# A ring of seven split half tiles instead of six, with other operands and another order at the norms

## The chip, the cores and the metric

The kernel runs on one core of a Trainium2 chip. The metric is the device time of one execution in microseconds (us). Engines are named as in the profile: PE is TensorE (PEld its weight loads), DVE is VectorE, ACT is ScalarE, POOL is GpSimd, and SP issues most of the transfers.

## The reference

One decoder layer over 256 tokens of width 2048, all in float32. Three sublayers, each followed by a layer norm over `ALPHA * x + sublayer(x)`:

```python
x = layer_norm(ALPHA * x + 0.5 * swiglu_ffn(x, ffn1...), ln1_g, ln1_b)      # 2048 -> 5632 -> 2048
u = x @ w_in + b_in                                                         # 2048 -> 3328
q, k, v, conv_in = split(u)
attn_out = sliding_window_attention_with_sinks(q, k, v, attn_sinks)         # 16 heads, 2 KV heads, window 128
conv_out = conformer_conv_group(conv_in, ...)                               # GLU, causal depthwise conv of 31, norm, swish
x = layer_norm(ALPHA * x + concat(attn_out, conv_out) @ w_out + b_out, ln2_g, ln2_b)
x = layer_norm(ALPHA * x + 0.5 * swiglu_ffn(x, ffn2...), ln3_g, ln3_b)
```

where `layer_norm` takes mean and variance over the 2048 features of a token, and `swiglu_ffn` is `(silu(x @ w_gate) * (x @ w_up)) @ w_down`.

## The kernel before

**Numbers.** Each float32 matrix is split into two parts that the matmul takes: `hi`, a rounded copy (written by ACT), and `lo`, what is left (`raw - hi`, written by DVE, or by POOL for some tiles). A product is then three matmuls (`mm3`, L383): hi with hi, hi with lo, lo with hi.

**Weights.** All weights stream from HBM once, in transfers of 1 MB, each two half tiles of 128 by 1024. `RAW_BUFS = 4` raw buffers hold them. `Steps.split` (L113) makes hi and lo of the next half tile. The results live in a ring of `RING` pairs of buffers; `Steps.ahead` (L138) stops the split of half tile n when `n >= min(used + LEAD, done + RING)`: not more than `LEAD` ahead of the last half tile taken, and not before `RING` older ones were released. `pooled` is the set of half tiles whose lo POOL makes; `POOL_FIRST` lists those at the start of the input projection and of the second FFN.

**Order.** The instructions of every engine run in the order in which the program issues them. `Steps.step` (L166) is called after each half tile's matmuls. It counts a clock `now`, runs the pieces of work that `at(delay, work)` had set for this step (first those without `after`), then splits up to two half tiles, then runs the pieces with `after`. So an engine's queue holds, for one step, first the due work, then the split.

**Tokens.** 256 tokens are two blocks of 128. Output projections (`tokens_by`, L417) go chunk by chunk of 512 features: PSUM sums for both blocks, `evacuate` (L262) adds them to the residual `xt` on DVE and takes `bn_stats`. At the end of a sublayer block 1 lags behind: for the last `SKEW` half tiles only block 0's matmuls are issued at first, `finish(0)` issues block 0's norm, then follow block 1's matmuls of the held half tiles, one step each, block 1's last evacuation, and `finish(1)`.

**Norms.** For the two inner norms `finish` is `norm_to_features` (L292). On DVE: `bn_aggr`, `rsqrt` by Newton rounds (waiting xcat subtractions are put between the rounds), then four chunks `z = (xt - mean) * r` (L325). Then, at the steps listed in `LN_AT` as (delay, chunk, what): what 0 is `turn`, four transposes of a chunk on PE into PSUM (L302); what 1 is `scale`, gain and bias on ACT (L310) and the rounded copy into xcat's hi part, also on ACT (L311); what 2 is `settle`, the subtraction for xcat's lo part on DVE (L312). The last norm is `norm_to_rows` (L364), which stores to the output.

**After the norm.** `token_group` (L396) takes the first half tiles of the next weights, `skew` of them first for block 0 alone, then the same for block 1, then the rest for both. In the mixer its result holds k, v and the first two pairs of q heads (`kvq`, L590). Then come features (`in_c`, `in_q`), attention by pairs of heads, the gated convolution input (`glu`, L658), and the convolution as chains of 31 taps on DVE, which are issued so long as a modelled backlog of DVE is below `CAP`. While the mixer and the second FFN start, `residuals` (L333) rebuilds the scaled residual from `xt`; it loads rows of gain, bias and output bias, broadcast over the partitions, into `BC` buffers (`row_chunk`, L257) through SP's queue.

Of the kernel before, what the change touches and what calls it, by code (L numbers as in the profile page):

```python
# [9 lines left out]
F32 = mybir.dt.float32  # L10
# [3 lines left out]
AF = mybir.ActivationFunctionType  # L14
ALU = mybir.AluOpType
# [3 lines left out]
P = 128  # L19
D = 2048  # L20
S = 256
# [8 lines left out]
CK = 31  # L30
# [5 lines left out]

RAW_BUFS = 4
EARLY = 4
RING = 6
LEAD = 5  # L40
SKEW = 6
BC = 6
ORDER = "ccqqccqqccqqcc"
CAP = 4.0
CONV_AT = (1, 3, 1)
HB = 5
POOL_FIRST = (0, 1, 2, 4)
POOL_SPAN = (20, 84)
POOL_SHARE = (4, 7)
ZB = 5  # L50

LN_AT = ((5, 0, 0), (5, 0, 1), (6, 1, 0), (6, 2, 0), (6, 1, 1), (6, 3, 0), (6, 0, 2), (6, 2, 1), (7, 3, 1), (7, 0, 2), (7, 0, 2), (8, 0, 2))
ATT = (1, 1, 2, 2, 4, 6, 7)
ENGINES = {getattr(mybir.EngineType, e) for e in ("PE", "DVE", "Activation", "Pool", "SP")}

# [1 line left out]
class Steps:  # L57
# [55 lines left out]
    def split(self):  # L113
# [5 lines left out]
        else:  # L119
            if n not in self.ready:  # L120
                self.ready[n] = [
                    self.pool.tile([P, 1024], F32R, tag=t, name=f"{t}{n}", bufs=RING) for t in ("hi", "lo")
                ]
# [57 lines left out]
def hybrid_layer(  # L181
# [3 lines left out]
    nc = tc.nc  # L185
# [7 lines left out]
    psC = ctx.enter_context(tc.tile_pool(name="psC", bufs=1, space=PSUM))  # L193
# [14 lines left out]
    first = 2 * len(sources)  # L208
# [16 lines left out]
    ident = const.tile([P, P], F32, name="ident")  # L225
# [5 lines left out]
    for lo_, base, mult, step in ((0, 0, 1, -1), (P, -1, -1, 1), (2 * P, 0, 1, -1)):  # L231
        nc.gpsimd.affine_select(
            out=mask[:, lo_ : lo_ + P], in_=mask[:, lo_ : lo_ + P], compare_op=ALU.is_ge,
            fill=NEG, base=base, pattern=[[step, P]], channel_multiplier=mult,
        )
    bias = const.tile([P, 26], F32, name="bias")
# [4 lines left out]
    xt = act.tile([P, 2, D], F32, name="xt")  # L241
# [50 lines left out]
    def norm_to_features(b, stats, par, gcol, xc):  # L292

        mv, r = par[:, b, 0:2], par[:, b, 2:3]
        zs, tps = [], []

        def turn(c):
            if c % 2 == 0:
                tps.append(psA.tile([P, 2, 4, P], F32, tag="gu", name=f"tp{b}_{c}"))
            tp = tps[c // 2][:, c % 2]  # L300
            for k in range(4):
                nc.tensor.transpose(tp[:, k], zs[c][:, k * P : (k + 1) * P], ident)  # L302

        def scale(c):
            tp = tps[c // 2][:, c % 2]
            k4, cols = slice(4 * c, 4 * c + 4), slice(b * P, (b + 1) * P)
            full = zs[c].rearrange("p (k n) -> p k n", k=4)
            for k in range(4):
                g, be = (lnp[:, gcol + n, 4 * c + k : 4 * c + k + 1] for n in range(2))
                nc.scalar.activation(full[:, k], tp[:, k], AF.Identity, scale=g, bias=be)  # L310
            nc.scalar.copy(xc[:, k4, 0, cols], full)  # L311
            waiting.append(lambda: nc.vector.tensor_tensor(  # L312
                out=xc[:, k4, 1, cols], in0=full, in1=xc[:, k4, 0, cols].bitcast(F32), op=ALU.subtract
            ))

        def settle(most=9):
            for _ in range(min(most, len(waiting))):
                waiting.pop(0)()

        nc.vector.bn_aggr(out=mv, in_=stats[b].rearrange("p c s -> p (c s)"))  # L320
        rsqrt(mv[:, 1:2], r, waiting)
        settle()
        for c in range(NC_):
            z = act.tile([P, 512], F32, tag="z", name=f"z{b}_{c}", bufs=ZB)
            nc.vector.tensor_scalar(  # L325
                out=z, in0=xt[:, b, c * 512 : (c + 1) * 512], scalar1=mv[:, 0:1], scalar2=r,
                op0=ALU.subtract, op1=ALU.mult,
            )
            zs.append(z)
        for n, c, what in LN_AT:  # L330
            st.at(n, lambda c=c, what=what: (turn(c) if what == 0 else scale(c) if what == 1 else settle(1)))

    def residuals(par, row, more, eng, start, every):  # L333
# [218 lines left out]


    x2 = mixer(tc, nc, locals())


# [17 lines left out]
def mixer(tc, nc, env):  # L574
    act, small, psA, psB, st = env["act"], env["small"], env["psA"], env["psB"], env["st"]
    xt, x1, mm3, tokens_by = env["xt"], env["x1"], env["mm3"], env["tokens_by"]
    bias, cw_sb, cp_sb, nsink, psink = (env[k] for k in ("bias", "cw_sb", "cp_sb", "nsink", "psink"))
    ident, ident_b, mask = env["ident"], env["ident_b"], env["mask"]
    blk = [slice(b * P, (b + 1) * P) for b in range(2)]

    with tc.tile_pool(name="mix", bufs=1) as pool:
# [4 lines left out]

        bk = act.tile([P, 512], F32, tag="bc", name="bk", bufs=BC)
        nc.sync.dma_start(bk, env["b_tok"].partition_broadcast(P))
        grp = env["token_group"](x1, SKEW)
        kvq = pool.tile([P, 2, 512], F32, name="kvq")  # L590
        kT = pool.tile([P, S], F32, name="kT")
        qTs = {t: pool.tile([P, S], F32, tag="qT", name="qT", bufs=3) for t in range(2)}
        v = [kvq[:, b, P : 2 * P] for b in range(2)]
        for b in range(2):
            nc.vector.tensor_tensor(out=kvq[:, b], in0=grp[b], in1=bk, op=ALU.add)

        def turn_first():
            tq = psA.tile([P, 2, 512], F32, tag="gu", name="tq")
            for b in range(2):
                for n, col in enumerate((0, 2, 3)):  # L600
                    nc.tensor.transpose(
                        tq[:, n // 2, (n % 2) * S + b * P : (n % 2) * S + (b + 1) * P],
                        kvq[:, b, col * P : (col + 1) * P], ident,
                    )
            nc.scalar.copy(kT, tq[:, 0, :S])
            nc.scalar.copy(qTs[0], tq[:, 0, S:])
            nc.scalar.copy(qTs[1], tq[:, 1, :S])
            attend(0)
            st.at(3, lambda: attend(1))
# [47 lines left out]

        def glu(i, ps):  # L658
            hc = hcs[i % HB]
            sg = pool.tile([P, S], F32, tag="sg", name="sg", bufs=2)  # L660
            nc.scalar.activation(sg, ps[:, S:], AF.Sigmoid, bias=bias[:, 18 + i : 19 + i])
            nc.vector.scalar_tensor_tensor(
                out=hc[:, CK - 1 :], in0=ps[:, :S], scalar=bias[:, 10 + i : 11 + i], in1=sg,
                op0=ALU.add, op1=ALU.mult,
            )
            st.vector(0.4)
            todo.append((i, hc))
# [83 lines left out]
        for kind in ORDER:  # L751
            ps = psB.tile([P, 512], F32, tag="acc", name=f"in_{kind}")
# [79 lines left out]
def _layout(inputs):  # L832

    import numpy as np

    f = {k: np.asarray(v) for k, v in inputs.items()}
    x = f["x"][0]

    def cols(w, n):
        return w.reshape(KT, P, n, P).transpose(2, 1, 0, 3).reshape(n, P, KT * P)  # L840

    def rows_of(w):
        n = w.shape[0] // (4 * P)
        m = w.shape[1] // 512
        return w.reshape(n, 4, P, m, 512).transpose(3, 0, 2, 1, 4).reshape(m, n, P, 2048)

    def up(g, u):
        return np.stack([cols(g, JT), cols(u, JT)], axis=1)

    def up_tok(g, u):  # L850
        return rows_of(np.concatenate([g[:, : JT0 * P], u[:, : JT0 * P]], axis=1))[0]

    heads = np.stack([np.arange(NT), np.arange(NT) + NT], axis=1)
    qcols = (heads.reshape(-1)[:, None] * HD + np.arange(HD)).reshape(-1)
    order = np.concatenate([qcols, np.arange(1024, 3328)])
    w_in, b_in = f["w_in"][0][:, order], f["b_in"][0][order]
    win = cols(w_in, 26)
    seq, nc_, nq = [], 0, 2
    for kind in ORDER:
        if kind == "c":  # L860
            seq += [10 + nc_, 18 + nc_]
            nc_ += 1
        else:
            seq.append(nq)
            nq += 1
    first = np.concatenate([np.arange(1024, 1280), np.arange(2 * P)])
    w_out = f["w_out"][0]
    w_out = np.concatenate([w_out[qcols], w_out[1024:]], axis=0)
    return {
        "xT": x.T.reshape(KT, P, S).transpose(1, 0, 2),  # L870
        "x": x,
        "wt1": up_tok(f["ffn1_w_gate"][0], f["ffn1_w_up"][0]),
        "wu1": up(f["ffn1_w_gate"][0], f["ffn1_w_up"][0]),
        "wd1": rows_of(f["ffn1_w_down"][0]),
        "win": np.concatenate([rows_of(w_in[:, first])[0], win[seq]]),
        "wout": rows_of(w_out),
        "wt2": up_tok(f["ffn2_w_gate"][0], f["ffn2_w_up"][0]),
        "wu2": up(f["ffn2_w_gate"][0], f["ffn2_w_up"][0]),
        "wd2": rows_of(f["ffn2_w_down"][0]),
        "rows": np.stack([f[k][0] for k in ("ln1_g", "ln1_b", "b_out", "ln2_g", "ln2_b", "ln3_g", "ln3_b")]),  # L880
        "ln_cols": np.stack(
            [f[k][0].reshape(KT, P).T for k in ("ln1_g", "ln1_b", "ln2_g", "ln2_b")], axis=1
        ),
        "b_in": b_in.reshape(26, P).T,
        "b_tok": b_in[first],
        "sinks": np.stack([f["attn_sinks"][0].reshape(2, NT).T] * 2, axis=1),
        "cw": f["conv_dw_w"][0].T.reshape(NT, P, CK).transpose(1, 0, 2),
        "cpar": np.stack([f[k][0].reshape(NT, P).T for k in ("conv_dw_b", "conv_ln_g", "conv_ln_b")], axis=1),
    }
# [19 lines left out]
```

## Time and profile before

| | us |
|---|---|
| median of 3 runs (1784.53 to 1787.3) | 1785.87 |
| profiled execution, its own time | 1784.28 |
| its span, first to last instruction | 1782.5 |
| PE busy | 1747.7 |
| DVE busy | 1054.7 |
| ACT busy | 830.5 |
| POOL busy | 141.8 |
| all waits of PE that the trace lists, the start's 6.0 among them | 21.9 |

The mean granted clock of TensorE is 0.995. The first inner norm lies near 730 to 765 us, the second near 1023 to 1060 us, the convolution between them. In rows of the timeline the first number is the start in us, the second the duration, a bracket at the end tells how long the engine had stood idle and what released it. A row with x4 merges four instructions; its duration is from the first start to the last end. In rows of waits the numbers are the total, how often, and the longest.

### The profile page before, as it was taken

Reading aid. Unit: us, or ns where it says so; the run is one execution under the profiler, and the core shown is the slowest. Engines: PE = TensorE matmul, PEld = TensorE weight load, DVE = VectorE, ACT = ScalarE, POOL = GpSimd, SP = SyncE. Lnnn points to the kernel's source line nnn. Section 1 sums busy time; section 2 is a strip of 40 time slices with the busy share of each in tenths; the row PEclk is TensorE's granted clock in tenths of the full one; section 3 lists DMA queues with packets and bytes.
Section 4 is the critical chain, followed back from the end, with each engine's and each line's share of the span. In section 5 each row is a group of like instructions: output and inputs, shape, how many; then the busy total and the mean of one; then the engine's idle time right before and its main releaser. Section 6 shows DMA issues by size and latency. Waiting matters only on the chain.

```text
span 1782.5 us, 23512 instructions
## 1 busy us (share of the span) xinstructions
PE 1747.7 (98%) x9550; PEld 1512.8 (85%) x9550; DVE 1054.7 (59%) x1386; ACT 830.5 (47%) x1145; POOL 141.8 (8%) x82
## 2 busy tenths in 40 slices
PE   8999999999999999999998999999999999999997
PEld 6888888888888888789997778888888888888885
DVE  5555555445555555658889676755555445555546
ACT  5544444334444433575653474544443434444441
POOL 0000000000000000205654420000000000000000
PEclk9999999999999999999999999999999999999998
DMA  8655555555555555445544445655555555555651
GB/s 313 237 189 190 190 189 208 190 193 183 189 190 189 190 208 192 145 164 176 182 145 166 165 165 179 226 190 191 190 207 189 191 187 189 190 189 189 239 209 48
DMA packets 52092, 336.48 MB, mean 189 GB/s; under 512 B 6288, under 2 KB 6416, under 8 KB 13072
## 3 DMA queue, kind: packets, MB, share of 16 engines
q1 hardware_dynamic: 51984, 334.98, 53.7%
q8 instruction: 75, 1.23, 0.3%
q14 instruction: 33, 0.27, 0.0%
HBM read 332.86 MB, written 2.10 MB: 188 GB/s over the span
## 4 chain that ended last, share of the span: by engine, by line
PE 92%; DVE 4%; DMA 2%; ACT 1%; issue 1%; SPq 0%; DVEq 0%; ACTq 0%
PE gu L492 32%; PE gu L501 17%; PE acc L384 10%; PE acc L385 10%; PE acc L386 10%; PE in_c L384 2%; PE in_c L385 2%; PE in_c L386 2%; DMA rb<-in_rows 2%; PE grp L386 1%; PE grp L385 1%; PE grp L384 1%; DVE lo L128 1%; DVE z L325 1%; PE in_q L384 1%
## 5 line engine op out<-in xcount | busy, mean ns | idle before, releaser
L128 DVE TENSOR_TENSOR lo<-raw,hi 128x1024 fp32r<-128x1024 f32 (+1 forms) x569 | 695.3, 1238 | 520.1 <-issue 285.3
L126 ACT CAST hi<-raw 128x1024 fp32r<-128x1024 f32 (+1 forms) x614 | 633.4, 1047 | 335.2 <-PE acc L386 319.6
L492 PE MATMUL gu<-xcat,hi 128*128 128x512 f32 x2688 | 626.0, 390 | 0.5 <-ACT hi L126 0.5
L492 PEld LDWEIGHTS gu<-xcat,hi 128*128 128x128 f32 x2688 | 499.3, 188 | 101.2 <-ACT hi L126 1.0
L501 PEld LDWEIGHTS gu<-xcat,lo 128*128 128x128 f32 x2688 | 333.6, 192 | 6.5
L501 PE MATMUL gu<-xcat,lo 128*128 128x256 f32 x2688 | 335.6, 283 | 0.0
L384 PE MATMUL acc<-hi,hh 128*128 128x512 f32 x704 | 274.6, 390 | 0.0
L385 PE MATMUL acc<-lo,hh 128*128 128x512 f32 x704 | 274.4, 390 | 0.0
L386 PE MATMUL acc<-hi,hl 128*128 128x512 f32 x704 | 274.3, 390 | 0.0
L514 ACT COPY corr<-gu 128x512 f32<-128x512 f32 x84 | 49.3, 586 | 438.5 <-PE gu L501 438.5
L128 POOL TENSOR_TENSOR lo<-raw,hi 128x1024 fp32r<-128x1024 f32 x45 | 112.0, 2498 | 808.3 <-ACT hi L126 808.2
L386 PEld LDWEIGHTS acc<-hi,hl 128*128 128x128 f32 x704 | 132.5, 188 | 27.7
L384 PEld LDWEIGHTS acc<-hi,hh 128*128 128x128 f32 x704 | 132.5, 188 | 27.5
L385 PEld LDWEIGHTS acc<-lo,hh 128*128 128x128 f32 x704 | 132.5, 188 | 26.8
L515 DVE TENSOR_TENSOR both<-gu,corr 128x512 f32<-128x512 f32 x84 | 58.0, 691 | 84.2 <-ACT corr L514 84.2
L653 DVE SCALAR_TENSOR_TENSOR conv<-hc,cw_sb,conv 128x256 f32<-128x256 f32 x232 | 93.4, 479 | 3.2 <-ACT conv L649 3.2
L384 PE MATMUL in_c<-xcat,hi 128*128 128x256 f32 x256 | 73.9, 289 | 0.0
L386 PE MATMUL in_c<-xcat,lo 128*128 128x256 f32 x256 | 72.4, 283 | 0.0
L385 PE MATMUL in_c<-xcat,hi 128*128 128x256 f32 x256 | 72.4, 283 | 0.0
L265 DVE SCALAR_TENSOR_TENSOR xt<-acc,xt 128x512 f32<-128x512 f32 x48 | 32.9, 689 | 57.0 <-PE acc L386 57.0
L384 PE MATMUL acc<-hi,mh 128*128 128x512 f32 x128 | 51.2, 400 | 6.9 <-DVE xt L265 4.6
L384 PEld LDWEIGHTS in_c<-xcat,hi 128*128 128x128 f32 x256 | 49.0, 191 | 2.4 <-issue 2.3
(125 smaller groups left out, 1122.2 us busy)
## 6 DMA issues: line engine op xcount, KB each, us to landing
raw<-in_wu SPq DMA_DIRECT2D x168, 1024.0 KB, 4.8
raw<-in_wd SPq DMA_DIRECT2D x88, 1024.0 KB, 4.8
raw<-in_win SPq DMA_DIRECT2D x26, 1024.0 KB, 4.9
raw<-in_wout SPq DMA_DIRECT2D x16, 1024.0 KB, 4.8
raw<-in_wt SPq DMA_DIRECT2D x4, 1024.0 KB, 4.8
raw<-in_wt SPq DMA_DIRECT2D x6, 512.0 KB, 6.8
xt<-in_x SPq DMA_DIRECT2D x2, 1024.0 KB, 7.5
rg<-in_rows SPq DMA_DIRECT2D x8, 256.0 KB, 5.1
```

The costliest lines, as they stand in the source:

```text
L126: nc.scalar.copy(hi, raw)
L128: eng.tensor_tensor(out=lo, in0=raw, in1=hi.bitcast(F32), op=ALU.subtract)
L265: nc.vector.scalar_tensor_tensor(out=y, in0=ps, scalar=factor, in1=y, op0=ALU.mult, op1=ALU.add)
L325: nc.vector.tensor_scalar(out=z, in0=xt[:, b, c * 512 : (c + 1) * 512], scalar1=mv[:, 0:1], scalar2=r, op0=ALU.subtract, op1=ALU.mult,)
L384: nc.tensor.matmul(ps, s_hi, m_hi, start=start, stop=False)
L385: nc.tensor.matmul(ps, s_hi, m_lo, start=False, stop=False)
L386: nc.tensor.matmul(ps, s_lo, m_hi, start=False, stop=stop)
L492: nc.tensor.matmul(gu[:, m, :], parts[n4][0][:, q * P : (q + 1) * P], xc[:, k].rearrange("p a n -> p (a n)"), start=k == 0, stop=False,)
L501: nc.tensor.matmul(gu[:, m, S:], parts[n4][1][:, q * P : (q + 1) * P], xc[:, k, 0, :], start=False, stop=k == KT - 1,)
L514: nc.scalar.copy(corr, gu[:, :, S:])
L515: nc.vector.tensor_tensor(out=both, in0=gu[:, :, :S], in1=corr, op=ALU.add)
L653: nc.vector.scalar_tensor_tensor(out=acc if k < CK - 1 else cv[:, i], in0=hc[:, k : k + S], scalar=cw_sb[:, i, k : k + 1], in1=acc, op0=AL ...
```

## The change

- The ring holds seven pairs instead of six, the lead is six instead of five, and block 1 lags by seven half tiles instead of six.
- `POOL_FIRST` loses half tile 4; VectorE makes its lo.
- In `norm_to_features`, r is copied into a tile in PSUM, and z is made by `scalar_tensor_tensor` with that tile, broadcast, as second operand.
- The last chunk of a norm is scaled by VectorE (four `tensor_scalar` from PSUM) instead of ScalarE.
- `LN_AT` has a list of its own for each block; block 0's starts one step earlier.
- Row buffers fall from six to five, z buffers from five to four. The group's result is kept in two tiles, k and q in a buffer of the attention's ring and v in a smaller tile of its own; the columns of the first weights are reordered to suit. The sigmoid of `glu` is written to its target in place.

```diff
-RING = 6
-LEAD = 5
-SKEW = 6
-BC = 6
+RING = 7
+LEAD = 6
+SKEW = 7
+BC = 5
...
-POOL_FIRST = (0, 1, 2, 4)
+POOL_FIRST = (0, 1, 2)
...
-ZB = 5
-
-LN_AT = ((5, 0, 0), (5, 0, 1), (6, 1, 0), (6, 2, 0), (6, 1, 1), (6, 3, 0), (6, 0, 2), (6, 2, 1), (7, 3, 1), (7, 0, 2), (7, 0, 2), (8, 0, 2))
+ZB = 4
+
+LN_AT = (
+    ((4, 0, 0), (4, 0, 1), (5, 1, 0), (5, 1, 1), (5, 0, 2), (6, 2, 0), (6, 3, 0), (6, 2, 1), (6, 1, 2), (7, 3, 1), (7, 2, 2), (8, 3, 2)),
+    ((5, 0, 0), (5, 0, 1), (6, 1, 0), (6, 1, 1), (6, 0, 2), (7, 2, 0), (7, 3, 0), (7, 2, 1), (7, 1, 2), (8, 3, 1), (8, 2, 2), (9, 3, 2)),
+)
...
+        rp = psC.tile([P, 1], F32, tag="conv", name=f"rp{b}")
...
-                nc.scalar.activation(full[:, k], tp[:, k], AF.Identity, scale=g, bias=be)
+                if c < 3:
+                    nc.scalar.activation(full[:, k], tp[:, k], AF.Identity, scale=g, bias=be)
+                else:
+                    nc.vector.tensor_scalar(
+                        out=full[:, k], in0=tp[:, k], scalar1=g, scalar2=be, op0=ALU.mult, op1=ALU.add
+                    )
...
+        nc.vector.tensor_copy(rp, r)
...
-            nc.vector.tensor_scalar(
-                out=z, in0=xt[:, b, c * 512 : (c + 1) * 512], scalar1=mv[:, 0:1], scalar2=r,
+            nc.vector.scalar_tensor_tensor(
+                out=z, in0=xt[:, b, c * 512 : (c + 1) * 512], scalar=mv[:, 0:1], in1=rp.to_broadcast([P, 512]),
                 op0=ALU.subtract, op1=ALU.mult,
             )
...
-        for n, c, what in LN_AT:
+        for n, c, what in LN_AT[b]:
...
-        kvq = pool.tile([P, 2, 512], F32, name="kvq")
+        kq = pool.tile([P, 2, 3 * P], F32, tag="pr", name="kq", bufs=2)
+        vs = pool.tile([P, 2, P], F32, name="vs")
...
-            nc.vector.tensor_tensor(out=kvq[:, b], in0=grp[b], in1=bk, op=ALU.add)
+            nc.vector.tensor_tensor(out=kq[:, b], in0=grp[b][:, : 3 * P], in1=bk[:, : 3 * P], op=ALU.add)
+            nc.vector.tensor_tensor(out=vs[:, b], in0=grp[b][:, 3 * P :], in1=bk[:, 3 * P :], op=ALU.add)
...
-            sg = pool.tile([P, S], F32, tag="sg", name="sg", bufs=2)
-            nc.scalar.activation(sg, ps[:, S:], AF.Sigmoid, bias=bias[:, 18 + i : 19 + i])
+            h = hc[:, CK - 1 :]
+            nc.scalar.activation(h, ps[:, S:], AF.Sigmoid, bias=bias[:, 18 + i : 19 + i])
             nc.vector.scalar_tensor_tensor(
-                out=hc[:, CK - 1 :], in0=ps[:, :S], scalar=bias[:, 10 + i : 11 + i], in1=sg,
-                op0=ALU.add, op1=ALU.mult,
+                out=h, in0=ps[:, :S], scalar=bias[:, 10 + i : 11 + i], in1=h, op0=ALU.add, op1=ALU.mult,
             )
```

More of the change, by code (lines that the diff above doesn't have):

```diff
@@ L589, in mixer @@
         grp = env["token_group"](x1, SKEW)
-        kvq = pool.tile([P, 2, 512], F32, name="kvq")
+        kq = pool.tile([P, 2, 3 * P], F32, tag="pr", name="kq", bufs=2)
+        vs = pool.tile([P, 2, P], F32, name="vs")
         kT = pool.tile([P, S], F32, name="kT")
         qTs = {t: pool.tile([P, S], F32, tag="qT", name="qT", bufs=3) for t in range(2)}
-        v = [kvq[:, b, P : 2 * P] for b in range(2)]
+        v = [vs[:, b] for b in range(2)]
         for b in range(2):
-            nc.vector.tensor_tensor(out=kvq[:, b], in0=grp[b], in1=bk, op=ALU.add)
+            nc.vector.tensor_tensor(out=kq[:, b], in0=grp[b][:, : 3 * P], in1=bk[:, : 3 * P], op=ALU.add)
+            nc.vector.tensor_tensor(out=vs[:, b], in0=grp[b][:, 3 * P :], in1=bk[:, 3 * P :], op=ALU.add)
         def turn_first():
@@ L599, in turn_first @@
             for b in range(2):
-                for n, col in enumerate((0, 2, 3)):
+                for n in range(3):
                     nc.tensor.transpose(
                         tq[:, n // 2, (n % 2) * S + b * P : (n % 2) * S + (b + 1) * P],
-                        kvq[:, b, col * P : (col + 1) * P], ident,
+                        kq[:, b, n * P : (n + 1) * P], ident,
                     )
@@ L865, in _layout @@
             nq += 1
-    first = np.concatenate([np.arange(1024, 1280), np.arange(2 * P)])
+    first = np.concatenate([np.arange(1024, 1152), np.arange(2 * P), np.arange(1152, 1280)])
     w_out = f["w_out"][0]
```

## The prediction

> **What bounds the kernel now.** I read the page first: busy shares, then the chain that ended last.
>
> ```profile
> PE 1747.7 (98%) x9550; PEld 1512.8 (85%) x9550; DVE 1054.7 (59%) x1386; ACT 830.5 (47%) x1145; POOL 141.8 (8%) x82
> PE 92%; DVE 4%; DMA 2%; ACT 1%; issue 1%; SPq 0%; DVEq 0%; ACTq 0%
> ```
>
> TensorE bounds it, and its matmuls stay as they are. So the change can win or lose only where TensorE stands still. Next, the waits of TensorE alone:
>
> ```profile
> PE grp L384 <- ACT hi L126: 6.0, 1, 6.0
> PE tp L302 <- DVE z L325: 4.8, 4, 1.9
> PE acc L384 <- DVE xt L265: 4.6, 1, 4.6
> PE acc L384 <- ACT mh L804: 2.3, 1, 2.3
> ...
> PE gu L492 <- ACT hi L126: 0.5, 1, 0.5
> ```
>
> The first is the start. The waits on z are the two inner norms, which the change works on. The 4.6 and 2.3 lie in the convolution's stage. The timeline of the first norm, engine by engine:
>
> ```profile
> 730.09 0.39 PE L384 MATMUL acc<-hi,hh 128*128 128x512 f32 x1
> 731.45 0.39 PE L384 MATMUL acc<-hi,hh 128*128 128x512 f32 x1
> 738.14 0.63 PE L302 MATMUL tp<-ident,z 128*128 128x128 f32 x4 [0.52 <-DVE z L325]
> 740.64 1.19 PE L302 MATMUL tp<-ident,z 128*128 128x128 f32 x8 [1.87 <-DVE z L325]
> 750.67 0.65 PE L302 MATMUL tp<-ident,z 128*128 128x128 f32 x4
> 732.78 7.43 POOL L128 TENSOR_TENSOR lo<-raw,hi 128x1024 fp32r<-128x1024 f32 x3 [692.04 <-ACT hi L126]
> 733.90 0.21 DVE L288 TENSOR_SCALAR par<-rs_t,par 128x1 f32<-128x1 f32 x1
> 734.15 6.80 DVE L325 TENSOR_SCALAR z<-xt,par 128x512 f32<-128x512 f32 x4
> 740.87 1.21 DVE L128 TENSOR_TENSOR lo<-raw,hi 128x1024 fp32r<-128x1024 f32 x1
> 742.01 0.68 DVE L312 TENSOR_TENSOR xcat<-z,xcat 128x512 fp32r<-128x512 f32 x1
> 744.43 0.69 DVE L265 SCALAR_TENSOR_TENSOR xt<-acc,xt 128x512 f32<-128x512 f32 x1 [1.75 <-PE acc L386]
> 746.50 1.50 DVE L312 TENSOR_TENSOR xcat<-z,xcat 128x512 fp32r<-128x512 f32 x1
> 750.06 1.92 DVE L325 TENSOR_SCALAR z<-xt,par 128x512 f32<-128x512 f32 x4
> 752.50 1.22 DVE L128 TENSOR_TENSOR lo<-raw,hi 128x1024 fp32r<-128x1024 f32 x1
> 736.28 1.50 ACT L310 ACTIVATE z<-tp,lnp 128x128 f32<-128x128 f32 x4 [0.86 <-PE tp L302]
> 737.82 0.62 ACT L311 CAST xcat<-z 128x512 fp32r<-128x512 f32 x1
> 738.35 1.04 ACT L126 CAST hi<-raw 128x1024 fp32r<-128x1024 f32 x1
> 739.29 1.50 ACT L310 ACTIVATE z<-tp,lnp 128x128 f32<-128x128 f32 x4
> ```
>
> Read it so. Block 1's held matmuls begin at 730.09; one half tile is 1.36 us (to 731.45). Block 0's four z take 6.80 us beside POOL's three lo, block 1's four only 1.92 after POOL is done: TensorE waits 0.52 and 1.87 for the slow ones. Then block 1 is evacuated at 744.43, its z starts at 750.06, its first transposes at 750.67, just in time. From held start to those transposes: 20.58 us. The second norm has the same shape, 20.39 us:
>
> ```profile
> 1022.97 0.39 PE L384 MATMUL acc<-hi,mh 128*128 128x512 f32 x1
> 1043.36 0.66 PE L302 MATMUL tp<-ident,z 128*128 128x128 f32 x4
> ```
>
> **The change part by part.** All steps below are those of one norm, in the first norm's clock; a sum of row durations along each engine's queue, which keeps the program's order (the rows above stand in the order of the code).
>
> *z with a PSUM operand.* Rows that bear on it: the evacuation is the same instruction with one PSUM input.
>
> ```profile
> L325 DVE TENSOR_SCALAR z<-xt,par x16: 533/542/2603, 734.1 to 1044.1; 128x512 f32<-128x512 f32 x16
> L265 DVE SCALAR_TENSOR_TENSOR xt<-acc,xt x48: 672/691/692, 308.1 to 1770.3; 128x512 f32<-128x512 f32 x48
> L287 DVE TENSOR_SCALAR rs_t<-par,rs_w x18: 259/269/275, 732.5 to 1775.8; 128x1 f32<-128x1 f32 x18
> L786 DVE TENSOR_SCALAR cv<-tk,cmv,cr x4: 800/806/809, 975.6 to 981.5; 128x512 f32<-128x512 f32 x4
> ```
>
> L265 never exceeds 692 ns, whatever POOL does, while z reaches 2603. So z becomes 0.69 us, four pipelined 2.6 instead of 6.80; alone (block 1) it loses 0.7. The Trainium skill, "VectorE: DVE Perf Modes", section "Why PSUM operands drop a tier", says a PSUM operand rules out the fast two-port mode, so fp32 runs at the plain rate; by it alone the sixteen z would lose 16 x 0.15 = 2.4 us of VectorE time. That speaks against the change and the 542 against 691 agree, but block 0's 6.80 shows the larger price of the port. The copy of r into PSUM costs 0.14 to 0.27 (small rows); I take 0.2. r is done at 734.11, so z0 ends near 735.07.
>
> *Lag of seven, first transposes at 4.* Three held half tiles end at 730.09 + 4.08 = 734.17; the first transposes then wait for z0 until 735.1: a new stall of 0.9. After it no transposes of block 0 wait: all seven held half tiles end at 742.3 (seven of 1.36, the stall, and sixteen transposes of 0.11 by the eight at 740.64, whose 1.19 holds the full length of one).
>
> *Ring and lead; one tile fewer on POOL; last chunk on VectorE.* This is the part that decides. Before, the lead of five stops the split of the sixth half tile, and tile 4's lo is POOL's: only one lo and one xcat stand on VectorE between block 0's z and block 1's evacuation. Now tiles 3, 4 and 5 are all split there, by VectorE, in this order: xcat0, lo3, xcat1, lo4, four scales, xcat2, lo5, evacuation. Each lo waits for its hi, and each hi stands on ScalarE behind a scale and a cast. ScalarE's period is 3.01 us (scale at 736.28, cast, hi, next scale at 739.29). From its first scale at 735.74: hi2 737.8, hi3 740.8 (done 741.9), hi4 743.9 (done 744.9). VectorE idles for lo3 until 741.9, for lo4 until 744.9; lo4 ends its turn at 746.1; four scales of 128 columns, 0.27 to 0.81 each by L287 and L786, nearer the short one in width, 0.3 taken: 747.2; then ScalarE's cast 0.53, hi5 1.05, lo5 1.14: 750.0. There the evacuation starts, 7.7 us after block 1's matmuls ended.
>
> Evacuation to z took 750.06 - 744.43 = 5.63 before, with two xcat in between; now one is left (less 1.50, which POOL had stretched) and the copy comes in (0.24): 4.4, and z itself 0.7, so z is there at 755.2. Block 1's transposes are due after seven held and four group half tiles, at 742.3 + 5.45 = 747.7. TensorE stands there until 755.3, some 7.6 us. Bounds: with scales of 0.81 it is 9.6; with lo3 to lo5 out of the way it is 0.
>
> Against before: held start to those transposes 25.25, less 1.36 for the extra half tile that now lies inside, is 23.9: +3.3 in the first norm, +3.5 in the second. What follows them is 12 group half tiles in both.
>
> *The clock after the stall.* After a stall of 4.63 us TensorE restarted slowly:
>
> ```profile
> 946.78 0.77 PE L384 MATMUL acc<-hi,mh 128*128 128x512 f32 x1 [4.63 <-DVE xt L265]
> 949.48 0.47 PE L384 MATMUL acc<-hi,mh 128*128 128x512 f32 x1
> 741.40:744.70 3.30, 3.30 (x11) 2.62 (x10) 1.55 (x3) 2.84 (x7) 0.00 (x0) 0.51 0.57 184
> 1034.00:1037.00 3.00, 2.43 (x14) 1.76 (x13) 2.97 (x5) 2.65 (x7) 0.00 (x0) 1.00 0.30 120
> ```
>
> Six matmuls took 2.70 instead of 1.36: 1.34 lost. Before's first norm paid this too (granted clock 0.51 after its two waits), the second did not (1.00); both are inside the 20.58 and 20.39. After 7.6 us of stall I charge 1.34 in each norm (bounds 0 and 1.7, half of the 3.30 us window): +2.7. "TensorE: Matmul & The Clock Gate", section "What's actually happening", in the Trainium skill ties the half clock to a whole idle window of about 3.4 us; by it a 7.6 us stall must be followed by one, an estimated 1.7 each, and the clock after 0.52 and 1.87 should not have dropped, which the 0.51 contradicts.
>
> *Tail.* Block 0's last norm now starts one half tile earlier.
>
> ```profile
> 1769.20 0.39 PE L386 MATMUL acc<-hi,hl 128*128 128x512 f32 x1
> 1770.26 0.68 DVE L265 SCALAR_TENSOR_TENSOR xt<-acc,xt 128x512 f32<-128x512 f32 x1
> ```
>
> TensorE's end is 1769.59; the last evacuation waits until 1770.26 only because VectorE is still at block 0. With 1.36 more room it starts at 1769.63: -0.6.
>
> *Second FFN's first tile.* The 0.5 wait on hi goes with one more tile of lead: -0.5 (between 0 and -0.5).
>
> *Costs of nothing.* Five row buffers: each third row load now waits for POOL's multiply of the chunk before.
>
> ```profile
> 845.03 0.35 SPq L259 DMA_DIRECT2D ro<-in_rows  x1
> 852.00 24.11 SPq L108 DMA_DIRECT2D raw<-in_win  x4
> 849.40 1.31 POOL L357 TENSOR_TENSOR xt<-xt,rg 128x512 f32<-128x512 f32 x1
> ```
>
> In the worst chunk that holds SP's queue from 845.03 to 850.7; the weight load queued behind goes out at 852.00 anyway; without that cover it would be some 6 us late, inside the four raw buffers. The split of k, q and v costs VectorE two more instructions of some 0.2 behind the group, where TensorE is in the next features. The sigmoid written in place saves a buffer; its target's taps ended long before. Four z buffers: block 1 takes each after block 0's xcat, which VectorE's order gives already.
>
> *Convolution's stage.* 4.6 + 2.3 + 1.3 of clock hang on VectorE's queue there; the shifted lead moves single lo (1.2) before or behind the evacuation: bounds -8.2 and +2.4, taken 0, since the queue's content stays.
>
> **Sum.** 3.3 + 3.5 + 2.7 - 0.6 - 0.5 = +8.4 on the profiled execution's 1784.28 (span 1782.5), which is 1.6 under the median of 1785.87: 1792.7.
>
> **Rivals.** *Faster: the evacuation isn't held up.* If block 1's evacuation starts within 0.2 us of its last matmul, z is in time; what remains is 0.9 per norm. Before lost 20.58 - 10 x 1.36 - 16 transposes or 1.8 = 5.2, and 5.0: 10.2 - 1.8 + 1.1 gives -9.5, 1774.8. For it: z drops from 6.80 to 2.6 for sure, and ScalarE is relieved of 1.5. Against: three lo on VectorE and three scales ahead of hi5 on ScalarE. It decides at an evacuation lag of some 3 us: below, the norms gain.
>
> *No change: half the lag.* If the lag is 3 to 4 us, the stall (3.5) with 0.9 and less clock equals the 5 lost now: within 1784 to 1787. It needs ScalarE to be quicker by 1 us in each of its periods, which no row shows.
>
> *The convolution's stage decides.* If its waits vanish, 8.2 go: the first case becomes 1784.5; if they grow by 2.4, 1795.1. Folded into the ranges.
>
> **How the numbers follow.** Chance of the stall as walked 0.70 (own range 1787 to 1798: below, the clock's 2.7 and 3 of the convolution's 8.2 fall away; above, scales of 0.81 add 4.0 and the dearer clock 0.7); half lag 0.10; faster 0.20. A measurement tells some 0.2% (3.6 us) from no change. Slower 0.70, same 0.10, faster 0.20. The range reaches into the faster case, to 1776, and up to 1799.
>
> **What would show it.** Right: PE waits at block 1's transposes for z, 7 us or more in each norm, longest of the PE waits; L265 before it begins over 6 us after block 1's last matmul, behind a lo that waited for ACT hi; z near 0.69 everywhere; waits of 0.9 at block 0's first transposes and none at the others; last evacuation 0.05 behind TensorE's end. Wrong: if lo4 and lo5 come behind the evacuation on VectorE, if ScalarE makes hi3 to hi5 ahead of its scales, or if the convolution's waits move by more than 4.

## The result, and the profile after

The changed kernel is slower: 1796.29 us median of 5 runs (1795.56 to 1796.54) against 1786.37 of 5 runs of the kernel before beside them, ratio 1.0059 [1.0047, 1.0070]. Its profiled execution took 1796.31 us (span 1794.5), 12.0 more than the one shown of before; the medians differ by 9.9, since before's profiled execution lies 2.1 under its median. The accounts below are between the two profiled executions.

The page of the changed kernel, busy times and the chain that ended last:

```profile
PE 1751.3 (98%) x9550; PEld 1516.6 (85%) x9550; DVE 1057.8 (59%) x1410; ACT 825.1 (46%) x1129; POOL 136.3 (8%) x80
PE 92%; DVE 4%; ACT 2%; issue 1%; DMA 1%; POOL 0%; SPq 0%; DVEq 0%; POOLq 0%; ACTq 0%
```

The number of matmuls is the same, and shares of a whole span say nothing here. TensorE's waits do (line numbers have moved: transposes L306, z L336, evacuation L268):

```profile
PE tp L306 <- DVE z L336: 15.9, 4, 7.1
PE grp L395 <- ACT hi L129: 6.0, 1, 6.0
PE zt L806 <- DVE cv L798: 2.8, 1, 2.8
PE acc L395 <- DVE xt L268: 2.4, 2, 1.2
PE acc L395 <- DVE cv L666: 1.0, 1, 1.0
PE acc L395 <- ACT mh L816: 0.6, 1, 0.6
```

The waits on z went from 4.8 to 15.9. The convolution's 4.6 and 2.3 became five shorter waits, the last four rows. The first norm of the changed kernel, in the timeline of TensorE, VectorE and ScalarE:

```profile
728.72 0.39 PE L395 MATMUL acc<-hi,hh 128*128 128x512 f32 x1
733.87 0.63 PE L306 MATMUL tp<-ident,z 128*128 128x128 f32 x4 [0.91 <-DVE z L336]
741.36 0.39 PE L397 MATMUL acc<-hi,hl 128*128 128x512 f32 x1
754.29 1.11 PE L306 MATMUL tp<-ident,z 128*128 128x128 f32 x4 [7.10 <-DVE z L336]
732.78 0.16 DVE L333 COPY rp<-par 128x1 f32<-128x1 f32 x1
732.98 2.72 DVE L336 SCALAR_TENSOR_TENSOR z<-xt,par,rp 128x512 f32<-128x512 f32 x4
736.73 0.69 DVE L321 TENSOR_TENSOR xcat<-z,xcat 128x512 fp32r<-128x512 f32 x1 [1.03 <-ACT xcat L320]
740.68 1.23 DVE L131 TENSOR_TENSOR lo<-raw,hi 128x1024 fp32r<-128x1024 f32 x1 [3.26 <-ACT hi L129]
741.82 0.69 DVE L321 TENSOR_TENSOR xcat<-z,xcat 128x512 fp32r<-128x512 f32 x1
743.68 1.23 DVE L131 TENSOR_TENSOR lo<-raw,hi 128x1024 fp32r<-128x1024 f32 x1 [1.17 <-ACT hi L129]
744.82 1.36 DVE L317 TENSOR_SCALAR z<-tp,lnp 128x128 f32<-128x128 f32 x4
747.81 1.23 DVE L131 TENSOR_TENSOR lo<-raw,hi 128x1024 fp32r<-128x1024 f32 x1 [1.03 <-ACT hi L129]
748.96 0.68 DVE L268 SCALAR_TENSOR_TENSOR xt<-acc,xt 128x512 f32<-128x512 f32 x1
753.48 2.72 DVE L336 SCALAR_TENSOR_TENSOR z<-xt,par,rp 128x512 f32<-128x512 f32 x4
739.61 1.04 ACT L129 CAST hi<-raw 128x1024 fp32r<-128x1024 f32 x1
742.61 1.04 ACT L129 CAST hi<-raw 128x1024 fp32r<-128x1024 f32 x1
```

Read VectorE's rows downward. The four z of block 0 take 2.72 us where they took 6.80. Then the queue stands three times for a hi that ScalarE hasn't made yet (3.26, 1.17, 1.03), and the evacuation of block 1 is the last in this queue: it starts at 748.96, although TensorE was done with block 1 at 741.36 + 0.39 = 741.75. It has no bracket, so it waited for nothing but its own engine. From there to z it is 4.52 us, and TensorE stands 7.10 us. The second norm, and TensorE's clock at both stalls (columns of the last two rows: window, length, busy time and count of PE, PEld, DVE, ACT and POOL, granted clock, DMA share, GB/s):

```profile
1029.46 0.39 PE L395 MATMUL acc<-hi,mh 128*128 128x512 f32 x1
1034.53 0.66 PE L306 MATMUL tp<-ident,z 128*128 128x128 f32 x4 [0.82 <-DVE z L336]
1054.97 1.11 PE L306 MATMUL tp<-ident,z 128*128 128x128 f32 x4 [7.10 <-DVE z L336]
...
749.28:759.52 10.24, 5.23 (x17) 4.36 (x18) 8.37 (x20) 2.79 (x7) 0.00 (x0) 0.50 0.36 128
1053.07:1059.89 6.82, 4.92 (x16) 4.14 (x17) 5.47 (x11) 2.47 (x6) 0.00 (x0) 0.50 0.11 47
```

Both stalls are 7.10 long. These two windows hold all of the half clock at the norms: in the microsecond ahead of each and behind each the granted clock is 1.00. It begins while TensorE stands still, and TensorE then works at half clock for 5.23 and 4.92 us.

### The profile page after: what moved, and what is told of

Read it like the earlier page. It is cut to its first block, busy times and chain, and to the rows that moved or that the text cites. A ratio compares the mean times of both kernels' runs of the same rounds, so it can differ in the third digit from the quotient of the medians.

```text
span 1794.5 us, 23447 instructions
## 1 busy us (share of the span) xinstructions
PE 1751.3 (98%) x9550; PEld 1516.6 (85%) x9550; DVE 1057.8 (59%) x1410; ACT 825.1 (46%) x1129; POOL 136.3 (8%) x80
## 4 chain that ended last, share of the span: by engine, by line
PE 92%; DVE 4%; ACT 2%; issue 1%; DMA 1%; POOL 0%; SPq 0%; DVEq 0%; POOLq 0%; ACTq 0%
PE gu L503 34%; PE gu L512 18%; PE acc L395 10%; PE acc L397 10%; PE acc L396 10%; PE in_c L395 1%; DVE conv L666 1%; PE in_c L397 1%; PE in_c L396 1%; PE grp L396 1%; PE grp L395 1%; PE grp L397 1%; ACT hi L129 1%; DVE lo L131 1%; DMA raw<-in_wt 0%
## 5 line engine op out<-in xcount | busy, mean ns | idle before, releaser
L131 POOL TENSOR_TENSOR lo<-raw,hi 128x1024 fp32r<-128x1024 f32 x43 | 107.3, 2498 | 861.0 <-ACT hi L129 854.0
L268 DVE SCALAR_TENSOR_TENSOR xt<-acc,xt 128x512 f32<-128x512 f32 x48 | 32.9, 690 | 58.4 <-PE acc L397 58.4
```

The costliest lines, as they stand in the source:

```text
L131: eng.tensor_tensor(out=lo, in0=raw, in1=hi.bitcast(F32), op=ALU.subtract)
L268: nc.vector.scalar_tensor_tensor(out=y, in0=ps, scalar=factor, in1=y, op0=ALU.mult, op1=ALU.add)
```

## The experiments

The theory: the three lo of half tiles 3 to 5, which the lead of six and the shorter `POOL_FIRST` put on VectorE, hold up block 1's evacuation; all else is small. The rivals: the loss lies in the z with a PSUM operand or in VectorE's scales, or in the lag and the ring as such. Each comparison is with runs of the kernel before on the same chip.

**a_pool6: POOL takes the lo of half tiles 3 to 5 too**

```diff
-POOL_FIRST = (0, 1, 2)
+POOL_FIRST = (0, 1, 2, 3, 4, 5)
```

> The changed kernel with the lo parts of half tiles 3, 4 and 5 at each norm on POOL too (POOL_FIRST 0 to 5). Theory: block 1's evacuation waits behind these three lo on VectorE, so it now starts about 2.3 us after block 1's last matmul instead of 7.4, the stall at block 1's transposes falls from 7.1 to about 2.7 in each norm and the half clock after it goes: 1796.3 less 2 x 4.4 and less some 3 of clock, 1784 to 1787. Rival (the lag of seven, the order of the transposes or ScalarE's chain alone makes the stall): the stall stays above 6, 1794 to 1797.

Measured 1785.24 us, ratio to before 1.0003 [0.9994, 1.0012]: one line gives the whole loss back. Rows of its first norm:

```profile
744.35 0.69 DVE L268 SCALAR_TENSOR_TENSOR xt<-acc,xt 128x512 f32<-128x512 f32 x1
749.85 0.43 PE L306 MATMUL tp<-ident,z 128*128 128x128 f32 x1 [2.29 <-DVE z L336]
```

The evacuation starts 2.2 us behind TensorE's last matmul of block 1 instead of 7.2, and the stall falls from 7.10 to 2.29. So the lo on VectorE are the cause.

**a_scale_act: the last chunk is scaled by ScalarE again**

```diff
-                if c < 3:
+                if c < 4:
```

> The changed kernel with the last chunk scaled on ScalarE as before. Theory: VectorE's four scales are only one link of the chain; without them the evacuation comes 1 us sooner, stall 6.1 to 6.7, 1794 to 1795.5. Rival (moving the scales to VectorE is what blocks the evacuation): the stall falls by 4 or more in each norm, 1785 to 1788.

Measured 1794.89, ratio 1.0053 [1.0039, 1.0066]. The stall is 6.00, the evacuation 6.1 behind TensorE instead of 7.2. The four scales (1.36 us of VectorE) cost the path 1.1 per norm; the time as a whole can't be told from the changed kernel's.

**a_plain_z: z from SBUF again, no copy of r**

```diff
-        rp = psC.tile([P, 1], F32, tag="conv", name=f"rp{b}")
...
-        nc.vector.tensor_copy(rp, r)
...
-            nc.vector.scalar_tensor_tensor(
-                out=z, in0=xt[:, b, ...], scalar=mv[:, 0:1], in1=rp.to_broadcast([P, 512]),
+            nc.vector.tensor_scalar(
+                out=z, in0=xt[:, b, ...], scalar1=mv[:, 0:1], scalar2=r,
```

> The changed kernel with z from two SBUF operands, no PSUM copy. Theory: block 0's z are slow again (6.8 us for four) and TensorE waits about 0.7 at a second chunk, but ScalarE's chain and the lo behind it set block 1's evacuation, so the stall at block 1's transposes shrinks by as much as the other waits grow: within 1 us of the changed kernel, 1795 to 1797.5. Rival A (the PSUM operand is what gains, and the stall hides it): slower by 4 to 10, 1800 to 1806. Rival B (the PSUM operand costs, 0.15 a piece and a copy): faster by 2 to 3, 1793 to 1794.

Measured 1797.29, ratio 1.0064 [1.0051, 1.0077]. Block 0's transposes wait 1.27 and 0.52, block 1's 6.47: what the PSUM operand wins at block 0 disappears in the stall behind it. So it isn't the loss, and it is no gain here either.

**b_psum_z_pool6, b_psum_z, b_pool6: the two edits on the kernel before, together and alone.** All three keep before's ring of six, lead, lag and `LN_AT`.

```diff
 # b_psum_z: z with the PSUM operand
+        rp = psC.tile([P, 1], F32, tag="conv", name=f"rp{b}")
+        nc.vector.tensor_copy(rp, r)
-            nc.vector.tensor_scalar(... scalar1=mv[:, 0:1], scalar2=r, ...)
+            nc.vector.scalar_tensor_tensor(... scalar=mv[:, 0:1], in1=rp.to_broadcast([P, 512]), ...)
 # b_pool6: six lo on POOL
-POOL_FIRST = (0, 1, 2, 4)
+POOL_FIRST = (0, 1, 2, 3, 4, 5)
 # b_psum_z_pool6: both
```

> The kernel before, ring and lag of six, with two things only: z with the PSUM operand and the lo parts of half tiles 0 to 5 on POOL. Theory: z no longer waits for POOL, and no lo but POOL's stands ahead of block 1's evacuation: of the 5 us lost in each norm some 1.3 are left, no half clock in the first: 1786.4 less 8, 1777 to 1780. Rival (more POOL work stretches VectorE's subtractions through the shared port, or the lag of six is too short): 1785 to 1789.

> The kernel before with z from the PSUM operand alone (POOL keeps half tiles 0, 1, 2, 4). Theory: the wait moves: block 0's z are done 4 us sooner, but VectorE then stands for lo of half tile 3 behind ScalarE's hi, POOL's half tile 4 stretches an xcat, and block 1's evacuation starts 1.4 us late; a stall of some 2.6 at block 1's transposes replaces the waits of 2.4 on block 0's z: 0.5 less per norm, and the half clock of the first norm (1.3) may go: 0 to 3 us faster than before. Rival (the slow z are the whole loss): 7 to 9 us faster.

> The kernel before with the lo parts of half tiles 0 to 5 on POOL and z as it was. Theory: without the PSUM operand z and the xcat subtractions wait for POOL at every turn; waits of 0.7, 2.1 and 2.1 at block 0's z and 1.7 at block 1's: 2 us more per norm, 2 to 6 us slower than before. Rival (taking lo off VectorE is what gains in the pair): 4 to 8 us faster.

| | us | ratio to before | waits of the transposes on z |
|---|---|---|---|
| both | 1776.76 | 0.9954 [0.9941, 0.9966] | 0.8 |
| PSUM operand alone | 1782.24 | 0.9986 [0.9977, 0.9995] | 4.9 |
| six on POOL alone | 1793.70 | 1.0051 [1.0037, 1.0065] | 12.0 |

One edit alone wins 2.7 us, the other loses 8.8, both together win 7.4, and that is the fastest kernel of this study. The gains are near what was expected (0 to 3, and some 8). The loss of six on POOL alone is above the 2 to 6 expected: its waits came much as expected (0.51, 1.87 and 1.77 at block 0's z and 1.91 at block 1's in the first norm), but the time from held start to block 1's transposes grew by 4.3 and 4.5 us in the two norms where 2 was reckoned. Block 0's z, POOL's work beside it, and block 1's evacuation, first in the kernel with six on POOL alone, then with both edits:

```profile
733.25 8.85 DVE L325 TENSOR_SCALAR z<-xt,par 128x512 f32<-128x512 f32 x4
731.87 9.93 POOL L128 TENSOR_TENSOR lo<-raw,hi 128x1024 fp32r<-128x1024 f32 x4 [692.61 <-ACT hi L126]
745.86 0.69 DVE L265 SCALAR_TENSOR_TENSOR xt<-acc,xt 128x512 f32<-128x512 f32 x1 [3.17 <-PE acc L386]
```

```profile
733.27 2.72 DVE L327 SCALAR_TENSOR_TENSOR z<-xt,par,rp 128x512 f32<-128x512 f32 x4
731.71 9.93 POOL L128 TENSOR_TENSOR lo<-raw,hi 128x1024 fp32r<-128x1024 f32 x4 [692.12 <-ACT hi L126]
739.59 0.69 DVE L265 SCALAR_TENSOR_TENSOR xt<-acc,xt 128x512 f32<-128x512 f32 x1 [0.23 <-PE acc L388]
745.41 0.65 PE L303 MATMUL tp<-ident,z 128*128 128x128 f32 x4 [0.39 <-DVE z L327]
```

POOL's four lo are the same 9.93 us. From SBUF alone, the four z take nearly as long as those four lo, as if each waited for one; with the PSUM operand they take 2.72, as everywhere, so the work can go to POOL at no cost to z. The Trainium skill, "SBUF — State Buffer", section "Who interferes with whom", says a VectorE instruction with at most one SBUF input and outside the two-port modes doesn't contend with GpSimd; 2.72 beside 8.85 agrees.

With the PSUM operand alone, z no longer holds up block 0, but a subtraction for xcat between the Newton rounds of block 1 meets the one lo that POOL has there, and block 1's transposes wait 2.47 and 2.42 for it:

```profile
743.77 2.78 DVE L313 TENSOR_TENSOR xcat<-z,xcat 128x512 fp32r<-128x512 f32 x1
743.60 2.39 POOL L128 TENSOR_TENSOR lo<-raw,hi 128x1024 fp32r<-128x1024 f32 x1 [4.53 <-ACT hi L126]
748.57 0.66 PE L303 MATMUL tp<-ident,z 128*128 128x128 f32 x4 [2.47 <-DVE z L327]
```

**a_lead5 and a_lead4_held: fewer half tiles ahead**

```diff
 # a_lead5
-LEAD = 6
+LEAD = 5
 # a_lead4_held: a lead of four from finish(0) to finish(1), six elsewhere
-        ... min(used + LEAD, done + RING)
+        ... min(used + self.lead, done + RING)
+        st.lead = 4        # before finish(0)
+        st.lead = LEAD     # after finish(1)
```

> The changed kernel with a lead of five everywhere (ring and lag stay at seven). Theory: half tile 5 is split behind block 1's evacuation, which comes 2.2 us sooner: stall 5 instead of 7.1, and a new wait of 0.6 for its lo: 1.7 less per norm, 1792 to 1794. If the lead is also what made the convolution's stage 2.3 us longer, that comes back too: 1790 to 1792, and the waits there are those of the kernel before. Rival (the lead has no part): 1796.

> The changed kernel with a lead of four from block 0's norm until block 1's norm is issued, six elsewhere, so that the splits of half tiles 4 and 5 come behind block 1's evacuation. Theory: the stall at block 1's transposes falls to about 2.7 and a new wait of 2.4 for lo of half tile 4 appears in the group: VectorE's work is only moved; 2.3 less per norm and less half clock, 1789 to 1792. Rival (order alone is to blame): the stall goes without a successor, 1782 to 1784.

a_lead5 measured 1790.0, ratio 1.0031 [1.0021, 1.0042]: one lo less in the queue, evacuation 5.0 behind TensorE, stall 4.87. The new wait of 0.6 that was expected for the lo put off doesn't show in its trace. a_lead4_held measured 1791.54, 1.0038 [1.0025, 1.0051]. There two lo are put off; the stall is short, but the work is missed right behind it. First a_lead5, then a_lead4_held:

```profile
751.37 1.11 PE L306 MATMUL tp<-ident,z 128*128 128x128 f32 x4 [4.87 <-DVE z L336]
...
749.03 0.66 PE L307 MATMUL tp<-ident,z 128*128 128x128 f32 x4 [2.41 <-DVE z L337]
752.14 0.80 PE L397 MATMUL grp<-lo,xcat 128*128 128x512 f32 x1 [2.22 <-DVE lo L132]
```

A lo that VectorE hasn't made before the evacuation is due after it. Putting off the last of the three brought no new wait and took 2.2 to 2.3 off the stall in each norm; putting off the one before it too took off another 2.5, but brought a wait of 2.22 and 1.92 on its lo. So delay helps as far as there is room behind the evacuation, and beyond that it only moves the wait.

**a_late: everything out of the evacuation's way.** Changed kernel with six lo on POOL, lead five, all scales on ScalarE, and the last scale and settles of block 0 one step later.

```diff
-LEAD = 6
+LEAD = 5
-HB = 5
+HB = 4
-POOL_FIRST = (0, 1, 2)
+POOL_FIRST = (0, 1, 2, 3, 4, 5)
-ZB = 4
+ZB = 5
-    (... (7, 3, 1), (7, 2, 2), (8, 3, 2)),
+    (... (8, 3, 1), (8, 2, 2), (9, 3, 2)),
-                if c < 3:
+                if c < 4:
```

> The changed kernel (ring and lag of seven, z with the PSUM operand, own order of each block) with everything taken away that stands ahead of block 1's evacuation: lo of half tiles 0 to 5 on POOL, all scales on ScalarE, block 0's last scale and settle steps one step later (behind the evacuation; five z buffers for it, four convolution inputs to make room), lead five. Theory: the evacuation starts within 0.2 us of block 1's last matmul, no stall of more than 1 us at block 1's transposes, the 0.9 at block 0's first transposes stays: as fast as the kernel before with PSUM z and POOL lo, 1775 to 1778 beside a kernel before of 1784 to 1786. Rival (a ring and lag of seven cost by themselves): 1782 or more.

Measured 1781.63, ratio 0.9986 [0.9977, 0.9995]: faster than before, but a miss, 3.6 us above the upper end expected.

```profile
740.86 0.69 DVE L268 SCALAR_TENSOR_TENSOR xt<-acc,xt 128x512 f32<-128x512 f32 x1 [1.12 <-PE acc L397]
742.93 2.83 DVE L321 TENSOR_TENSOR xcat<-z,xcat 128x512 fp32r<-128x512 f32 x1
747.55 2.72 DVE L336 SCALAR_TENSOR_TENSOR z<-xt,par,rp 128x512 f32<-128x512 f32 x4
748.35 0.66 PE L306 MATMUL tp<-ident,z 128*128 128x128 f32 x4 [2.09 <-DVE z L336]
742.81 2.40 POOL L131 TENSOR_TENSOR lo<-raw,hi 128x1024 fp32r<-128x1024 f32 x1 [0.59 <-DVE rs_v L281]
```

The evacuation is on time: it waited for TensorE, not TensorE for it. But the subtraction for xcat between the Newton rounds, which took 0.68 in the changed kernel with POOL idle, now stands beside a lo of POOL that started 0.12 us ahead of it, and takes 2.83, as in b_psum_z. Evacuation to z is 6.69 instead of 4.52, and the stall of 2.09 that comes of it is about that excess. Being on time at the evacuation isn't enough; the subtractions behind it, with both operands in SBUF, must be clear of POOL as well. The time lies nearer the rival's 1782 or more than the theory's 1778: a_late is some 5 us above b_psum_z_pool6, and beside the stalls it pays 0.91 and 0.83 at block 0's first transposes, which belong to the changed order. Whether a ring and lag of seven cost anything by themselves isn't separated by these runs.

**a_pool6_lead5 and b_cap3: the convolution's stage.** The first is a_pool6 with a lead of five. The second is b_psum_z_pool6 with a smaller modelled backlog of convolution taps.

```diff
 # a_pool6_lead5
-LEAD = 6
+LEAD = 5
 # b_cap3
-CAP = 4.0
+CAP = 3.0
```

> The changed kernel with lo of half tiles 0 to 5 on POOL and a lead of five. The norms are those of the same kernel with lead six (stall 2.3), since half tile 5's lo is POOL's either way. Theory: lead six costs the convolution's stage some 2 us (from the first in_c to the second norm 254.5 to 256.5 us with it, 252.3 to 254.0 without); that comes back: 1 to 3 us faster than with lead six, which ran at 1.0003 of the kernel before, and the wait for xt of 4.6 stands there again. Rival (row buffers, k and q split or the sigmoid in place make the stage longer): no change.

> The kernel before with PSUM z and POOL lo of half tiles 0 to 5, and the modelled backlog of convolution taps capped at 3 instead of 4. Theory: the wait of 4.6 for the evacuation in the convolution's stage is taps queued ahead of it on VectorE; with 1 us less of them it falls by about 1, but the chain ends later and the wait of 2.3 before the second half grows by as much: within 1.5 us of the same kernel with 4. Rival (the taps queue alone decides): 2 to 4 us faster.

a_pool6_lead5 measured 1783.55, 0.9994 [0.9985, 1.0003], against 1.0003 [0.9994, 1.0012] with lead six: the direction expected, though the intervals overlap. The wait for xt of 4.6 stands there again, and a wait of 1.0 for a hi came up in the second FFN. b_cap3 measured 1777.34, 0.9962 [0.9949, 0.9976], no different from 0.9954. Its waits moved:

```profile
PE zt L796 <- DVE cv L788: 5.9, 1, 5.9
PE acc L386 <- DVE xt L265: 1.1, 1, 1.1
```

The evacuation's wait fell from 4.6 to 1.1 and the 2.3 went, but 5.9 came up at the transposes behind the last taps: 6.9 before, 7.0 now. That the waits would only move was expected, where they would go was not. In this pair of kernels the order of VectorE's queue chooses where TensorE waits, not how long.

## Why the prediction came out as it did

The forecast was 1792.7 and slower; 1796.29 came, inside the range and inside the likeliest case's own 1787 to 1798, 3.6 above the point. The forecast put its +8.4 on before's profiled execution; between the medians the change is +9.9, between the profiled executions +12.0. Term by term, profiled execution against profiled execution. The rows that are still wanted for it, from the timelines of before and then of the changed kernel: the first matmul of the stage behind each norm, and of the changed kernel the end.

```profile
769.30 0.28 PE L384 MATMUL in_c<-xcat,hi 128*128 128x256 f32 x1
1061.96 3.79 PE L492 MATMUL gu<-xcat,hi 128*128 128x512 f32 x16
```

```profile
774.92 0.28 PE L395 MATMUL in_c<-xcat,hi 128*128 128x256 f32 x1
1075.45 3.79 PE L503 MATMUL gu<-xcat,hi 128*128 128x512 f32 x16
1781.84 0.39 PE L397 MATMUL acc<-hi,hl 128*128 128x512 f32 x1
1782.27 0.69 DVE L268 SCALAR_TENSOR_TENSOR xt<-acc,xt 128x512 f32<-128x512 f32 x1 [0.64 <-PE acc L397]
```

| term | predicted | measured | worked out |
|---|---|---|---|
| held start to block 1's transposes, norm 1 | +3.3 | +3.6 | 754.29 - 728.72 - 1.36 = 24.21, was 20.58 (the 1.36 is the extra held half tile) |
| the same, norm 2 | +3.5 | +3.8 | 1054.97 - 1029.46 - 1.36 = 24.15, was 20.39 |
| from there to the next stage, both norms | +2.7 | +3.9 | 20.63 and 20.48, were 18.63 and 18.60 |
| convolution's stage | 0 | +2.2 | first in_c to held start: 1029.46 - 774.92 = 254.54, was 1022.97 - 769.30 - 1.36 = 252.31 |
| second FFN's first tile | -0.5 | -0.9 | shift of 13.49 at its start, 12.64 at the last matmul; between them, at 1122.36, before waits 0.55 for a hi |
| tail | -0.6 | -0.6 | shift of 12.64 at the last matmul, 12.0 at the end |
| sum | +8.4 | +12.0 | |

**The stall.** The mechanism is as walked. VectorE's order was xcat, lo, xcat, lo, four scales, xcat, lo, evacuation; the evacuation started 20.2 us behind the held start where 19.9 was walked (748.96 - 728.72 against 750.0 - 730.09), and 7.2 us behind TensorE where 7.7 was predicted; evacuation to z is 4.52 where 4.4 was walked, and the stall 7.10 where 7.6 was. The step that was off is TensorE's own: its last matmul of block 1 ended 13.0 us behind the held start (741.75 - 728.72), where 12.2 was walked; beside the seven half tiles and the new stall, block 0's transposes and what stands between them took 2.6, where 1.8 was reckoned. So block 1's transposes came 0.3 later than walked, and the stall ahead of them is still 0.5 shorter. The other errors were small: z took 0.742 us, not 0.69, the copy 0.16, not 0.2, the four scales 1.36, not 1.1.

**Block 0.** The new stall of 0.9 at its first transposes came as 0.91 and 0.82, and none of the others waits for z (one waits 0.22 for ScalarE's z in each norm).

**The clock: the mis-sized term.** The charge of 1.34 per norm came from a stall of 4.63 us, with a bound of 1.7 from a window of 3.30 us. Behind 7.10 us TensorE worked at half clock for 5.23 and 4.92 us, half of which, 2.6 and 2.5, are lost by the clock alone, and 2.0 and 1.9 show in the rows. The bound was wrong: it took the length of one slow stretch for the longest there can be. The Trainium skill, "TensorE: Matmul & The Clock Gate", section "What's actually happening", by which the prediction estimated 1.7 each, fell short too. Of the 0.6 by which the rows show less than the clock, 0.2 is a wait for ScalarE behind block 1's first transposes that before has (0.21 and 0.22) and the changed kernel hasn't; the rest stays open.

**The convolution's stage: the other one.** Taken 0, within bounds of -8.2 and +2.4, it came at +2.2. TensorE's waits there sum to much the same (4.6, 2.3 and 0.3 before; 2.8, 2.4, 1.0, 0.6 and 0.5 after). Over the first 190.7 us of the stage the two kernels are level, with 1387 and 1388 matmuls; the 2.2 come up in its last 62 to 64 us, where the waits are 2.6 in before and 3.4 after, and where the changed kernel has a granted clock of 0.50 from 991.63 to 995.04 (before's such stretch, from 946.24, lies in the first part). The lead of six accounts for some 1.0 to 1.8 of it, by one profile each: 254.5 against 253.5 in a_lead5, 254.6 in a_pool6 against 252.8 in a_pool6_lead5. The rest isn't settled; the kernels with before's ring and lead show 252.3 to 254.0 themselves.

**The second FFN's first tile.** The wait of before went, as forecast, but a_lead5 hasn't got it either with a lead of five, so that one more tile of lead removed it isn't shown.

**The rivals.** "Faster: the evacuation isn't held up" put the point where the norms begin to gain at an evacuation lag of some 3 us. In a_pool6 it is 2.2 and the kernel stands level with before, and a_late, with none, gains 2.3 us, not 9.5. So that rival's price was too high for this lag and order: it left out that a lo on POOL can stretch an xcat subtraction between evacuation and z. b_psum_z_pool6, whose POOL is idle there in the first norm (from 741.64 to 743.35), comes near the price with 7.4. That is in part luck: both its xcat subtractions there, at 741.67 and 742.70, happen to fall into POOL's pause and take 0.68 each. "Half the lag" at no change is near what a_pool6 does, with an evacuation 2.2 us late and a stall of 2.29, but by POOL, not by a quicker ScalarE.

## What to carry to other kernels

Before a queue in program order gets more work "because the engine is idle there", list what stands in it between the event that another engine waits for and that event's end: here three lo, each of them waiting for a cast that itself stood behind other work, and TensorE stood twice for 7.1 us while VectorE was busy 59% of the span. Take two changes that share a resource apart and together: with both z from PSUM and the lo on POOL the kernel won 0.46%, with the lo on POOL alone it lost 0.51%. Delaying work helps only as far as there is room before it is due: one lo put off was free here, the second came back as a wait of about 2 us. Giving the work to another engine helped only where what was left on VectorE didn't meet that engine's work.

## What the runs showed of the hardware

- VectorE's z with one PSUM operand took 742 ns in the median of its 16 cases and never above 748, also beside POOL's lo; the same z with its data in SBUF alone took 533 to 2603 in the kernel before.

```profile
L336 DVE SCALAR_TENSOR_TENSOR z<-xt,par,rp x16: 742/742/748, 733.0 to 1056.2; 128x512 f32<-128x512 f32 x16
```

- The half clock isn't a fixed price per stall. The granted clock was 0.50 from 946.24 to 949.65 around the end of a stall of 4.63 us in the kernel before (3.41 us, 2.87 of them after TensorE restarted), and for 10.24 and 6.82 us around the ends of two stalls of 7.10 in the changed kernel (5.23 and 4.92 after the restart). Every such stretch that the thirteen traces record ahead of the last matmul lasted 3.41 us, or two or three times that. Nor does the length of a stall settle it: a_late stands 2.09 us in both norms, and its clock falls only in the second. The Trainium skill, "TensorE: Matmul & The Clock Gate", section "What's actually happening", gives about 3.4 us of sustained work until the full clock returns; the 5.23 and 4.92 here are longer than that.
